# Softmax sums spread by TensorE, and the merge's other loads issued by ScalarE, in a hybrid decoder layer

## The chip, the cores and the metric

The kernel runs on 1 core of one Trainium2 chip. The metric is the device time of one execution in microseconds (us), lower is better. A core has TensorE (PE, the matrix array; PEld are its weight loads), VectorE (DVE), ScalarE (ACT), GpSimd (POOL) and SyncE (SP), each with a queue that it works through in order, and 16 DMA engines that move data between DRAM and SBUF. SyncE computes nothing here; its queue issues transfers. ScalarE, too, can issue transfers from its queue, between its computations. A matrix product is written to PSUM, eight banks of 128 x 512 numbers; whoever reads a bank sets it free.

## What is computed

One decoder layer of a sequence of 1024 tokens of width 1024: a SwiGLU half step, two token mixers side by side (a gated delta rule, and sparse attention with 8 heads), their merge by sigmoid gates, the output projection, a second half step. Of the reference, cut to what this change touches:

```python
logits = jnp.einsum('bqhr,bqkr->bqhk', q_lat, c_sel) * (SA_DH ** -0.5) + bias
p = jax.nn.softmax(logits, axis=-1)
o_lat = jnp.einsum('bqhk,bqkr->bqhr', p, c_sel)
o_sa = jnp.einsum('bqhr,rhd->bqhd', o_lat, w_uv).reshape(B, Q_BLOCK, SA_W)
...
merged = jax.nn.sigmoid(gate_a) * o_dn + jax.nn.sigmoid(gate_b) * o_sa
x = x + merged @ w_o
```

All of it is in float32; the kernel makes a product of two float32 matrices from three products of their rounded parts (`mm3`: high x high, high x low, low x high).

## The kernel before

The stage in question is the sparse attention, from about 1610 to 1900 us. It goes over 8 heads, in pairs that share one load of value weights (w_uv, `attn_values`: eight products into vh and vl). For each head, query and key are projected from the latents (`attn_qk`, PSUM tag qk, products named pqk): weights w_uq and w_uk are loaded through the two slots of w_raw, cast to a high part by ScalarE and split by GpSimd (wa), multiplied, and evicted by ScalarE and VectorE (p). The call of `ahead()` at step 1 projects the next head while this one runs.

`attn_head` then takes the queries in four groups g of 256, in the order 0, 1, 3, 2. For a group: GpSimd adds the bias of near keys to a mask (nb); TensorE multiplies queries by keys (pl, three banks); VectorE adds the mask and takes the row maximum (a_mx, a_nm); ScalarE takes the exponential and sums each row (a_sum); TensorE transposes the probabilities in blocks (pp, two banks, tag pt); ScalarE and VectorE evict them in parts (ph, plo); TensorE multiplies them by the values (pao, one bank); ScalarE copies the result to osa. There the head's channel is on the partitions and the query along the row, while a_sum has the query on the partitions. So the reciprocal sums r of a half head (512 queries, 128 x 4 numbers) must be turned into a row and spread over all partitions.

`merge` does that after groups 1 and 2, once per half head. It loads three tiles of 128 x 512 with one buffer each: od (the other mixer's result, `odd`), zg and gb (gates, `zgd` and `gbd`). It stores r to DRAM (a_rd), and loads it back as a row for every partition (a_rb, one buffer). For the very last half head it uses TensorE instead: four diagonal matrices made by VectorE (a_d), multiplied by ones (a_rp). What `merge` returns, `done`, is called one group later for the first half and two groups later for the second: GpSimd multiplies od by zg, VectorE multiplies osa by the spread sums and gate, GpSimd adds both into the row merged[hd] (mr).

All these loads and the store leave from SyncE's queue, and so do the weights (line 1256), the near bias (line 584) and then w_o (line 132). The order of instructions on each engine is set when the program is built, by a scheduler that plays the program in a model of time; `issue_after` keeps an instruction from being put ahead of another one, and `high_priority` lets the projection go up to 1600 instructions ahead. After the heads the merged rows are split in two parts (mh by ScalarE, ml by VectorE and GpSimd), and the output projection follows (pwo).

Of the kernel before, what the change touches and what calls it, by code (L numbers as in the profile page):

```python
# [10 lines left out]
F32 = mybir.dt.float32  # L11
F32R = mybir.dt.float32r
# [3 lines left out]
ALU = mybir.AluOpType  # L16
# [4 lines left out]
P = 128  # L21
D = 1024
S = 1024
# [47 lines left out]
class Layer:  # L71
# [1188 lines left out]
    def attn_values(self, pair, p, ps):  # L1260
        nc = self.nc
        wh, wl = self.attn_weights(self.I["w_uv"][0][:, 2 * pair:2 * pair + 2, :].rearrange("r h d -> r (h d)"), 256, p, "wuv")
        vh = p.tile([P, NT, 256], F32R, name="vh", tag="vh", bufs=1)
        vl = p.tile([P, NT, 256], F32R, name="vl", tag="vl", bufs=1)
        for t in range(0, NT, 2):
            pv = ps.tile([P, 2, 256], F32, name="pav", tag="qk")
            for i in range(2):
                for k in range(2):
                    lh, ll = (x[2 + k][t // 4][:, ts((t + i) % 4, P)] for x in self.lat)
                    self.mm3(pv[:, i, :], lh, ll, wh[:, k, :], wl[:, k, :], k == 0, k == 1)  # L1270
            nc.scalar.copy(vh[:, t:t + 2, :], pv)
            nc.vector.tensor_sub(vl[:, t:t + 2, :], pv, vh[:, t:t + 2, :])
        return vh, vl
# [20 lines left out]

    def attn_head(self, hd, p, ps, qk, values, merged, ahead):
        nc = self.nc
# [4 lines left out]
        sums = self.stat.tile([P, NT], F32, name="a_sum")  # L1301
        osa = p.tile([P, S], F32, name="osa", tag="osa", bufs=2)
        for g in (0, 1, 3, 2):
            probs = []
            for b in (2 * g, 2 * g + 1):
# [24 lines left out]
            for j in range(0, 2 * g + 2, 2):  # L1330
# [3 lines left out]
                for i, (jj, b) in enumerate(blocks):  # L1334
                    nc.tensor.transpose(pt[:, ts(i, P)], probs[b][:, ts(jj, P)], self.ident)
                ph = p.tile([P, 512], F32R, name="ph", tag="ph", bufs=3)
# [3 lines left out]
                for i in range(2):  # L1340
                    a, b = (0, 256) if i == 0 else (256, n)
                    out = po[:, 0:256] if b - a == 256 else po[:, 128:256]
                    self.mm3(out, vh[:, j + i, hv], vl[:, j + i, hv], ph[:, a:b], pl_[:, a:b], j + i == 0, j + i == 2 * g + 1)
            nc.scalar.copy(osa[:, ts(g, 256)], po[:, 0:256])
            if g == 1:
                ahead()
            for late in self.outs:
                late[0] -= 1
            while self.outs and self.outs[0][0] == 0:
                with self.tc.issue_after(dve.ins):  # L1350
                    self.outs.pop(0)[1]()
            if g in (1, 2):
                out = self.merge(hd, g // 2, sums, osa, p, ps, merged)
                if hd == H - 1 and g == 2:
                    out()
                else:
                    self.outs.append([g, out])

    def merge(self, hd, h, sums, osa, p, ps, merged):
# [5 lines left out]
        nc.vector.tensor_scalar_mul(r, r, 0.5)  # L1365
        od, zg, gb = (p.tile([P, 512], F32, name=n, tag=n, bufs=1) for n in ("od", "zg", "gb"))
        v = ts(h, 512)
        for x, src in ((od, self.odd[hd][:, v]), (zg, self.zgd[hd][:, v]), (gb, self.gbd[hd][:, v])):
            nc.sync.dma_start(x, src)
        if hd == H - 1 and h == 1:  # L1370
            rb = ps.tile([P, 512], F32, name="a_rp", tag="pt")
            for t in range(4):
                d = p.tile([P, P], F32, name="a_d", tag="near", bufs=2)
                nc.vector.tensor_scalar_mul(d, self.ident, r[:, t:t + 1])
                nc.tensor.matmul(rb[:, ts(t, P)], lhsT=self.ones, rhs=d, start=True, stop=True)
        else:
            rd = self.dram.tile([512], F32, name="a_rd", tag="a_rd", bufs=2)
            nc.sync.dma_start(rd.rearrange("(t i) -> i t", i=P), r)
            rb = p.tile([P, 512], F32, name="a_rb", tag="a_rb", bufs=1)
            nc.sync.dma_start(rb, rd.partition_broadcast(P))  # L1380

        def done():
            nc.gpsimd.tensor_mul(od, od, zg)
            nc.vector.tensor_mul(osa[:, v], osa[:, v], rb)
            nc.vector.scalar_tensor_tensor(osa[:, v], gb, 1.0, osa[:, v], ALU.add, ALU.mult)
            nc.gpsimd.tensor_add(merged[:, v], od, osa[:, v])

        return done

# [139 lines left out]
    def mixer(self, hs):  # L1529
# [3 lines left out]
        with ExitStack() as km:  # L1533
# [79 lines left out]
            with ExitStack() as c:  # L1613
# [5 lines left out]

                def ahead():  # L1620
                    if len(qk) < H:
                        with self.tc.high_priority(offset=AHEAD):
                            qk.append(self.attn_qk(len(qk), (p, "wqk", 2), ps))

                for i in range(H):
                    if i % 2 == 0:
                        vals = self.attn_values(i // 2, p, ps)
                    self.attn_head(i, p, ps, qk[i], vals, raw[i], ahead)
                hs.close()
# [55 lines left out]
```

## Time and profile before

| | |
|---|---|
| time, 3 runs | 2646.43, 2651.6 (median), 2653.45 us |
| the profiled execution | 2654.08 us, span 2652.1 us |
| PE busy | 2519.1 us, 95% of the span |
| DVE, ACT, POOL busy | 66%, 45%, 37% |
| granted TensorE clock, mean | 0.971 of full |

The span goes from the first to the last instruction of the profiled execution. Busy shares are means over the whole kernel, most of which is other stages; what this change can move is in the 290 us of the attention. The granted clock is a share of 2.4 GHz; the array has two levels, 2.4 and 1.2 GHz, and a mean between them says for how much of a stretch each held.

### The profile page before, as it was taken

The numbers are of one execution on the slowest core, as the hardware profiler recorded it, in microseconds if no ns is written. First come the engines' busy times: TensorE is split into PE (matmuls) and PEld (weight loads), VectorE is DVE, ScalarE is ACT, GpSimd is POOL, SyncE is SP. The second block draws the span as 40 slices with busy tenths as digits, with TensorE's granted clock in tenths as the row PEclk, the third lists the DMA queues.
The fourth block names the chain that finished last, engine by engine and source line by source line (L and its number), as shares of the span: only waits on it lengthen the run. The fifth ranks groups of instructions, "written<-read, shape, count | busy, mean of one in ns | idle before, by whom it ended". The sixth has DMA issues, their size and how long they took to land.

```text
span 2652.1 us, 36132 instructions
## 1 busy us (share of the span) xinstructions
PE 2519.1 (95%) x12526; PEld 2054.9 (77%) x12526; DVE 1737.9 (66%) x3424; ACT 1198.3 (45%) x2338; POOL 970.9 (37%) x748
## 2 busy tenths in 40 slices
PE   6999999999999899989999999779898999999998
PEld 5788888888787688777778778678776888888886
DVE  7655555676555677999566866566668555546676
ACT  6444344333434665544368446445434434434333
POOL 5555444343434233332100002333446545543340
PEclk8999999999999899999999999889998999999999
DMA  5443346753444155445633323333632344347642
GB/s 168 136 143 129 113 146 219 255 194 101 120 114 122 41 140 139 115 124 123 200 124 116 124 82 74 82 76 78 200 111 94 102 143 143 127 150 263 224 151 75
DMA packets 375607, 356.67 MB, mean 134 GB/s; under 512 B 95417, under 2 KB 279553, under 8 KB 374401
## 3 DMA queue, kind: packets, MB, share of 16 engines
q1 hardware_dynamic: 371840, 348.60, 42.1%
q10 hardware_dynamic: 2304, 4.20, 0.4%
q0 software_dynamic: 1280, 1.57, 0.3%
q8 instruction: 99, 1.62, 0.3%
q14 instruction: 84, 0.68, 0.1%
HBM read 238.28 MB, written 116.01 MB: 134 GB/s over the span
## 4 chain that ended last, share of the span: by engine, by line
PE 40%; DVE 9%; DMA 6%; issue 2%; ACT 1%; POOL 1%; SPq 0%; DVEq 0%; POOLq 0%; ACTq 0%
PE pst L139 7%; PE pst L141 7%; PE pst L140 7%; PE pin L141 2%; PE pin L139 2%; PE pin L140 2%; DVE sb_p L1034 2%; DMA a_rd<-a_r 2%; DMA od<-odd 1%; PE pn L1221 1%; PE po L1230 1%; PE pv L1216 1%; DVE cv_y L923 1%; PE pq L1211 1%; PE pwo L141 1%
## 5 line engine op out<-in xcount | busy, mean ns | idle before, releaser
L140 PE MATMUL pst<-p,w_hi 128*128 128x512 f32 x992 | 392.1, 395 | 8.6 <-DVE p L112 8.5
L139 PE MATMUL pst<-p,w_hi 128*128 128x512 f32 x992 | 393.2, 397 | 4.1 <-ACT p L111 2.3
L141 PE MATMUL pst<-p,w_hi 128*128 128x512 f32 x992 | 391.3, 395 | 0.5 <-DVE w_hi L112 0.5
L139 PE MATMUL pin<-p,w_hi 128*128 128x512 f32 (+1 forms) x848 | 342.1, 405 | 6.0 <-DVE cv_y L923 4.2
L111 ACT CAST w_hi<-w_raw 128x512 fp32r<-128x512 f32 (+3 forms) x294 | 204.1, 695 | 311.7 <-PE pst L141 135.8
L140 PE MATMUL pin<-p,w_hi 128*128 128x512 f32 (+1 forms) x848 | 340.5, 402 | 0.5 <-DVE p L112 0.5
L141 PE MATMUL pin<-p,w_lo 128*128 128x512 f32 (+1 forms) x848 | 340.8, 402 | 0.0
L112 DVE TENSOR_TENSOR w_lo<-w_raw,w_lo 128x512 fp32r<-128x512 f32 (+1 forms) x196 | 188.3, 963 | 167.2 <-ACT w_lo L111 165.6
L140 PE MATMUL pst<-p,w_lo 128*128 128x512 f32 x744 | 292.7, 394 | 3.7 <-DVE p L112 3.7
L141 PE MATMUL pst<-p,w_lo 128*128 128x512 f32 x744 | 292.2, 393 | 1.2 <-DVE w_lo L112 1.2
L139 PE MATMUL pst<-p,w_lo 128*128 128x512 f32 x744 | 290.6, 396 | 0.5 <-ACT c L360 0.5
L140 PEld LDWEIGHTS pst<-p,w_hi 128*128 128x128 f32 x992 | 188.3, 190 | 53.9 <-DVE p L112 12.9
L139 PEld LDWEIGHTS pst<-p,w_hi 128*128 128x128 f32 x992 | 188.8, 190 | 47.3 <-ACT p L111 3.5
L141 PEld LDWEIGHTS pst<-p,w_hi 128*128 128x128 f32 x992 | 188.5, 190 | 43.0 <-DVE w_hi L112 1.3
L111 ACT CAST w_lo<-w_raw 128x512 fp32r<-128x512 f32 (+1 forms) x200 | 115.7, 582 | 207.4 <-PE pst L141 97.8
L139 PEld LDWEIGHTS pin<-p,w_hi 128*128 128x128 f32 (+1 forms) x848 | 161.6, 191 | 42.7 <-DVE cv_y L923 4.5
L141 PEld LDWEIGHTS pin<-p,w_lo 128*128 128x128 f32 (+1 forms) x848 | 161.5, 190 | 37.7 <-issue 3.8
L140 PEld LDWEIGHTS pin<-p,w_hi 128*128 128x128 f32 (+1 forms) x848 | 161.6, 191 | 37.5 <-issue 4.0
L373 DVE TENSOR_TENSOR c<-c,pst 128x512 f32<-128x512 f32 x132 | 89.9, 682 | 150.9 <-PE pst L141 118.1
L112 POOL TENSOR_TENSOR w_lo<-w_raw,w_hi 128x1024 fp32r<-128x1024 f32 (+1 forms) x43 | 107.0, 2488 | 199.4 <-ACT w_hi L111 189.4
L140 PEld LDWEIGHTS pst<-p,w_lo 128*128 128x128 f32 x744 | 140.7, 189 | 35.1 <-DVE p L112 4.9
L141 PEld LDWEIGHTS pst<-p,w_lo 128*128 128x128 f32 x744 | 140.7, 189 | 33.5 <-DVE w_lo L112 2.1
(427 smaller groups left out, 5393.8 us busy)
## 6 DMA issues: line engine op xcount, KB each, us to landing
p<-mixd SPq DMA_DIRECT2D x144, 256.0 KB, 5.4
w_raw<-in_w_in_dram SPq DMA_DIRECT2D x52, 512.0 KB, 4.1
w_raw<-in_ffn_wg_dram SPq DMA_DIRECT2D x44, 512.0 KB, 3.6
w_raw<-in_ffn_wu_dram SPq DMA_DIRECT2D x44, 512.0 KB, 4.0
mixd<-t_hi SPq DMA_DIRECT2D x72, 256.0 KB, 4.3
mixd<-t SPq DMA_DIRECT2D x72, 256.0 KB, 3.8
w_raw<-in_ffn_wd_dram SPq DMA_DIRECT2D x48, 384.0 KB, 4.1
actd<-c SPq DMA_DIRECT2D x70, 256.0 KB, 2.0
```

The source lines that it names most:

```text
L111: self.nc.scalar.copy(hi, raw)
L112: self.pin((self.nc.vector if engine == "vector" else self.nc.gpsimd).tensor_sub(lo, raw, hi))
L139: mm(ps, lhsT=wh, rhs=rh, start=first, stop=False, **kw)
L140: mm(ps, lhsT=wh, rhs=rl, start=False, stop=False, **kw)
L141: mm(ps, lhsT=wl, rhs=rh, start=False, stop=last, **kw)
L373: nc.vector.tensor_add(c[i, h], c[i, h], bank["y" if m == 1 else "z"])
L923: nc.vector.scalar_tensor_tensor(y[:, n:512], pps[h][:, 0:512 - n], cw[:, j:j + 1], y[:, n:512], ALU.mult, ALU.add)
L1034: nc.vector.tensor_mul(v, T[:, 0:i, 0:i].rearrange("p j c -> p c j"), L[:, None, 0:i, i].to_broadcast([P, i, i]))
L1211: nc.tensor.matmul(pq[:, i, :], lhsT=kq[:, h, ts(c, P)], rhs=old[:, h, :], start=True, stop=True)
L1216: nc.tensor.matmul(pv[r, i, :], lhsT=X[r, h, :], rhs=vb[r, h, :], start=True, stop=True)
L1221: nc.tensor.matmul(pn[:, i, :], lhsT=kd[r, h, :], rhs=vn[r, h, :], start=True, stop=True)
L1230: nc.tensor.matmul(po[r, i, :], lhsT=at[r, h, :], rhs=vn[r, h, :], start=True, stop=True)
```

## The change

The reciprocal sums no longer go through DRAM: `spread`, which the kernel has for its norms, makes four products of r (each column repeated 128 times, as the weights) with the identity, into a bank of tag pt (n_rb), from which VectorE multiplies osa. This is used for every half head, the last included. `merge` becomes a generator: its first step takes the reciprocals and issues the load of gb (now two buffers) from ScalarE's queue; its second, one group later, does the rest. The other mixer's part is a generator of its own, `other_branch`: it loads the whole row of odd for a head straight into the merged row, and the gate zg by halves (one buffer), from ScalarE's queue, and GpSimd multiplies in place, one group after each load. GpSimd then adds osa (for the last half head VectorE does). The tiles osa, vh and vl are cut into two and four, so that a part can be freed earlier.

```diff
--- before.py
+++ after.py
@@ -1260,16 +1260,15 @@
     def attn_values(self, pair, p, ps):
         nc = self.nc
         wh, wl = self.attn_weights(self.I["w_uv"][0][:, 2 * pair:2 * pair + 2, :].rearrange("r h d -> r (h d)"), 256, p, "wuv")
-        vh = p.tile([P, NT, 256], F32R, name="vh", tag="vh", bufs=1)
-        vl = p.tile([P, NT, 256], F32R, name="vl", tag="vl", bufs=1)
+        vh, vl = ([p.tile([P, 2, 256], F32R, name=n, tag=f"{n}{t}", bufs=1) for t in range(NT // 2)] for n in ("vh", "vl"))
         for t in range(0, NT, 2):
             pv = ps.tile([P, 2, 256], F32, name="pav", tag="qk")
             for i in range(2):
                 for k in range(2):
                     lh, ll = (x[2 + k][t // 4][:, ts((t + i) % 4, P)] for x in self.lat)
                     self.mm3(pv[:, i, :], lh, ll, wh[:, k, :], wl[:, k, :], k == 0, k == 1)
-            nc.scalar.copy(vh[:, t:t + 2, :], pv)
-            nc.vector.tensor_sub(vl[:, t:t + 2, :], pv, vh[:, t:t + 2, :])
+            nc.scalar.copy(vh[t // 2], pv)
+            nc.vector.tensor_sub(vl[t // 2], pv, vh[t // 2])
         return vh, vl

     def attn_qk(self, hd, p, ps):
@@ -1292,15 +1291,16 @@
             qk.append((hi, lo))
         return qk

-    def attn_head(self, hd, p, ps, qk, values, merged, ahead):
+    def attn_head(self, hd, p, ps, qk, values, merged, ahead, other):
         nc = self.nc
         near = self.near_tile(p, hd)
         (qh, ql), (kh, kl) = qk
         vh, vl = values
         hv = slice((hd % 2) * P, (hd % 2) * P + P)
         sums = self.stat.tile([P, NT], F32, name="a_sum")
-        osa = p.tile([P, S], F32, name="osa", tag="osa", bufs=2)
         for g in (0, 1, 3, 2):
+            if g in (0, 3):
+                osa = p.tile([P, 512], F32, name="osa", tag="osa", bufs=2)
             probs = []
             for b in (2 * g, 2 * g + 1):
                 W = (b + 1) * P
@@ -1332,7 +1332,7 @@
                 blocks = [(j, 0), (j, 1), (j + 1, 0), (j + 1, 1)] if j < 2 * g else [(j, 0), (j, 1), (j + 1, 1)]
                 n = len(blocks) * P
                 for i, (jj, b) in enumerate(blocks):
-                    nc.tensor.transpose(pt[:, ts(i, P)], probs[b][:, ts(jj, P)], self.ident)
+                    pe = nc.tensor.transpose(pt[:, ts(i, P)], probs[b][:, ts(jj, P)], self.ident)
                 ph = p.tile([P, 512], F32R, name="ph", tag="ph", bufs=3)
                 pl_ = p.tile([P, 512], F32R, name="plo", tag="plo", bufs=3)
                 nc.scalar.copy(ph[:, 0:n], pt[:, 0:n])
@@ -1340,21 +1340,21 @@
                 for i in range(2):
                     a, b = (0, 256) if i == 0 else (256, n)
                     out = po[:, 0:256] if b - a == 256 else po[:, 128:256]
-                    self.mm3(out, vh[:, j + i, hv], vl[:, j + i, hv], ph[:, a:b], pl_[:, a:b], j + i == 0, j + i == 2 * g + 1)
-            nc.scalar.copy(osa[:, ts(g, 256)], po[:, 0:256])
-            if g == 1:
-                ahead()
-            for late in self.outs:
-                late[0] -= 1
-            while self.outs and self.outs[0][0] == 0:
-                with self.tc.issue_after(dve.ins):
-                    self.outs.pop(0)[1]()
-            if g in (1, 2):
-                out = self.merge(hd, g // 2, sums, osa, p, ps, merged)
-                if hd == H - 1 and g == 2:
-                    out()
-                else:
-                    self.outs.append([g, out])
+                    self.mm3(out, vh[j // 2][:, i, hv], vl[j // 2][:, i, hv], ph[:, a:b], pl_[:, a:b], j + i == 0, j + i == 2 * g + 1)
+            act = nc.scalar.copy(osa[:, ts(g % 2, 256)], po[:, 0:256])
+            ahead(hd, g)
+            with self.tc.issue_after(dve.ins), self.tc.issue_after(act.ins), self.tc.issue_after(pe.ins):
+                for out in self.outs:
+                    next(out, None)
+                if g in (1, 2):
+                    out = self.merge(hd, g // 2, sums, osa, p, ps, merged)
+                    next(out)
+                    self.outs = self.outs[-1:] + [out]
+                other(hd, g)
+            if hd == H - 1 and g == 2:
+                for out in self.outs:
+                    for _ in out:
+                        pass

     def merge(self, hd, h, sums, osa, p, ps, merged):

@@ -1363,29 +1363,27 @@
         r = self.stat.tile([P, 4], F32, name="a_r")
         nc.vector.reciprocal(r, sums[:, ts(h, 4)])
         nc.vector.tensor_scalar_mul(r, r, 0.5)
-        od, zg, gb = (p.tile([P, 512], F32, name=n, tag=n, bufs=1) for n in ("od", "zg", "gb"))
         v = ts(h, 512)
-        for x, src in ((od, self.odd[hd][:, v]), (zg, self.zgd[hd][:, v]), (gb, self.gbd[hd][:, v])):
-            nc.sync.dma_start(x, src)
-        if hd == H - 1 and h == 1:
-            rb = ps.tile([P, 512], F32, name="a_rp", tag="pt")
-            for t in range(4):
-                d = p.tile([P, P], F32, name="a_d", tag="near", bufs=2)
-                nc.vector.tensor_scalar_mul(d, self.ident, r[:, t:t + 1])
-                nc.tensor.matmul(rb[:, ts(t, P)], lhsT=self.ones, rhs=d, start=True, stop=True)
-        else:
-            rd = self.dram.tile([512], F32, name="a_rd", tag="a_rd", bufs=2)
-            nc.sync.dma_start(rd.rearrange("(t i) -> i t", i=P), r)
-            rb = p.tile([P, 512], F32, name="a_rb", tag="a_rb", bufs=1)
-            nc.sync.dma_start(rb, rd.partition_broadcast(P))
-
-        def done():
-            nc.gpsimd.tensor_mul(od, od, zg)
-            nc.vector.tensor_mul(osa[:, v], osa[:, v], rb)
-            nc.vector.scalar_tensor_tensor(osa[:, v], gb, 1.0, osa[:, v], ALU.add, ALU.mult)
-            nc.gpsimd.tensor_add(merged[:, v], od, osa[:, v])
-
-        return done
+        last = hd == H - 1 and h == 1
+        gb = p.tile([P, 512], F32, name="gb", tag="gb", bufs=2)
+        nc.scalar.dma_start(gb, self.gbd[hd][:, v])
+        yield
+        rb = self.spread(r, p, ps, "pt")
+        nc.vector.tensor_mul(osa, osa, rb)
+        nc.vector.scalar_tensor_tensor(osa, gb, 1.0, osa, ALU.add, ALU.mult)
+        (nc.vector if last else nc.gpsimd).tensor_add(merged[:, v], merged[:, v], osa)
+
+    def other_branch(self, hd, p, merged):
+
+        nc = self.nc
+        nc.scalar.dma_start(merged, self.odd[hd])
+        for h in range(2):
+            v = ts(h, 512)
+            zg = p.tile([P, 512], F32, name="zg", tag="zg", bufs=1)
+            nc.scalar.dma_start(zg, self.zgd[hd][:, v])
+            yield
+            nc.gpsimd.tensor_mul(merged[:, v], merged[:, v], zg)
+            yield


     def out_proj(self, m, ps, after_tile, after_half):
@@ -1617,15 +1615,23 @@
                 raw = [mlp.tile([P, S], F32, name=f"mr{k}", tag=f"mr{k}") for k in range(NK)]
                 qk = self.qk

-                def ahead():
-                    if len(qk) < H:
+                others = [self.other_branch(k, p, raw[k]) for k in range(H)]
+                next(others[0])
+
+                def other(hd, g):
+                    for k, at in ((hd, (0, 1, 3)), (hd + 1, (2,))):
+                        if k < H and g in at:
+                            next(others[k], None)
+
+                def ahead(hd, g):
+                    if hd + 1 < H and g == 1:
                         with self.tc.high_priority(offset=AHEAD):
-                            qk.append(self.attn_qk(len(qk), (p, "wqk", 2), ps))
+                            qk.append(self.attn_qk(hd + 1, (p, "wqk", 2), ps))

                 for i in range(H):
                     if i % 2 == 0:
                         vals = self.attn_values(i // 2, p, ps)
-                    self.attn_head(i, p, ps, qk[i], vals, raw[i], ahead)
+                    self.attn_head(i, p, ps, qk[i], vals, raw[i], ahead, other)
                 hs.close()
                 mp = self.pool(ms, "merged", 1, "right")
                 hi, lo = ([mp.tile([P, S], F32R, name=f"{n}{k}", tag=f"{n}{k}") for k in range(NK)] for n in ("mh", "ml"))
```

What that does to the queues, at three places. SyncE's queue, around the load of the third pair of heads' value weights (w_uv); od, zg, gb, a_rd and a_rb are the merge's transfers. Before:

```order
L1369 DMA od<-odd 128x512
L1369 DMA zg<-zgd 128x512
L1380 DMA a_rb<-a_rd 128x512
L1369 DMA gb<-gbd 128x512
L1369 DMA od<-odd 128x512
L1378 DMA a_rd<-a_r 128x4x1
L1369 DMA zg<-zgd 128x512
L1256 DMA w_raw<-in_w_uv_dram 128x2x256
L1380 DMA a_rb<-a_rd 128x512
L1369 DMA gb<-gbd 128x512
L1256 DMA w_raw<-in_w_uq_dram 128x2x128
L1369 DMA od<-odd 128x512
```

and now:

```order
L1256 DMA w_raw<-in_w_uq_dram 128x2x128
L584 DMA near<-nb_wide 128x256
L1256 DMA w_raw<-in_w_uk_dram 128x2x128
L584 DMA near<-nb_wide 128x256
L1256 DMA w_raw<-in_w_uv_dram 128x2x256
L1256 DMA w_raw<-in_w_uq_dram 128x2x128
L1256 DMA w_raw<-in_w_uk_dram 128x2x128
L1256 DMA w_raw<-in_w_uq_dram 128x2x128
```

The weights and the near bias stay; nothing of the merge is between them any more.

ScalarE's queue, ahead of the cast of the same value weights (wa 128x512); vh, ph, osa and p are evictions, ACTIVATE with a_sum the exponentials. Before:

```order
L1344 COPY osa<-pao 128x256
L1327 ACTIVATE w_lo,a_sum<-w_lo,a_nm 128x768
L1288 ACTIVATE p_10_15129<-pqk 128x512
L1288 ACTIVATE p_10_15140<-pqk 128x512
L111 CAST wa<-w_raw 128x256
L1338 CAST ph<-pp 128x512
L1338 CAST ph<-pp 128x384
L1288 ACTIVATE p_10_15151<-pqk 128x512
L111 CAST wa<-w_raw 128x512
L1288 ACTIVATE p_10_15162<-pqk 128x512
```

and now:

```order
L1344 COPY osa<-pao 128x256
L1369 DMA gb<-gbd 128x512
L1379 DMA mr_14141<-odd 128x1024
L1383 DMA zg<-zgd 128x512
L1270 CAST vh<-pav 128x512
L1327 ACTIVATE w_hi,a_sum<-w_hi,a_nm 128x896
L1338 CAST ph<-pp 128x512
...
L111 CAST wa<-w_raw 128x512
L1287 ACTIVATE p_10_15182<-pqk 128x512
L111 CAST wa<-w_raw 128x256
L1344 COPY osa<-pao 128x256
L1369 DMA gb<-gbd 128x512
L1383 DMA zg<-zgd 128x512
```

Loads of gb, of a whole row of odd (into mr) and of zg now stand between an eviction and the next exponentials.

TensorE's queue, at one of the 16 spreads (n_rb), with the products of probabilities and values (pao) and logits (pl) around it. Now:

```order
L139 MATMUL pao<-ph,vh 128x256
L140 MATMUL pao<-plo,vh 128x256
L141 MATMUL pao<-ph,vl 128x256
L179 MATMUL n_rb<-ident,a_r 128x128 x4
L139 MATMUL pao<-ph,vh 128x256
L139 MATMUL pl<-p_10_15549,p_10_15527 128x384
L140 MATMUL pl<-p_11_15550,p_10_15527 128x384
L141 MATMUL pl<-p_10_15549,p_11_15528 128x384
```

Before, no product of this kind stood there; only the last half head had its four (a_rp).

## Rows read from the trace of the kernel before

**Rows 1.** The page's head.

```profile
span 2652.1 us, 36132 instructions
```

**Rows 2.** Stretches: us, busy us of each engine (instructions), PEclk, DMA share, GB/s.

```profile
core 0: us, PE busy (x) PEld busy (x) DVE busy (x) ACT busy (x) POOL busy (x), PEclk, DMA share, GB/s
1620.00:1660.00 40.00, 40.00 (x271) 36.51 (x270) 29.50 (x94) 23.53 (x54) 13.45 (x17) 1.00 0.29 60
1660.00:1680.00 20.00, 14.76 (x96) 13.28 (x94) 11.64 (x46) 8.02 (x21) 4.48 (x7) 0.83 0.15 46
1680.00:1700.00 20.00, 18.87 (x135) 17.28 (x133) 12.18 (x31) 12.21 (x26) 8.12 (x10) 1.00 0.39 102
1700.00:1720.00 20.00, 9.11 (x30) 7.13 (x31) 6.03 (x18) 5.02 (x13) 5.72 (x6) 0.57 0.37 90
1720.00:1770.00 50.00, 47.86 (x332) 43.22 (x330) 36.44 (x116) 27.59 (x64) 19.02 (x24) 1.00 0.35 75
1770.00:1790.00 20.00, 8.52 (x27) 6.90 (x28) 6.07 (x18) 5.02 (x13) 6.09 (x6) 0.59 0.32 79
1790.00:1810.00 20.00, 20.00 (x134) 18.32 (x134) 14.84 (x54) 11.81 (x29) 8.95 (x13) 0.99 0.28 73
1810.00:1850.00 40.00, 34.73 (x232) 30.84 (x230) 27.78 (x83) 19.74 (x45) 10.18 (x11) 0.96 0.37 73
1850.00:1880.00 30.00, 21.72 (x117) 17.71 (x116) 23.75 (x55) 18.15 (x36) 14.21 (x12) 0.89 0.33 88
```

**Rows 3.** TensorE's waits, 1600 to 1910: total us, times, longest us.

```profile
PE pqk L139 <- DVE p L1289: 22.2, 4, 9.1
PE pl L139 <- DVE a_mx L1322: 9.9, 3, 5.1
```

**Rows 4.** The chain that ended last, at the first long gap: start, us, what.

```profile
1698.59 3.21 DMA od<-odd
...
1701.99 1.24 POOL od L1383
1703.23 0.69 POOL wa L112
...
1703.94 9.19 DMA w_raw<-in_w_uv_dram
...
1715.04 0.79 PE pqk L139
```

**Rows 5.** Waits in SyncE's queue, 1600 to 1910: total us, times, longest us.

```profile
SPq L1369 <- POOL od L1383: 91.0, 15, 12.5
SPq L1380 <- DMA a_rd<-a_r: 85.2, 12, 11.2
```

**Rows 6.** Waits of the other engines, 1580 to 1910: total us, times, longest us.

```profile
POOL od L1383 <- DMA od<-odd: 62.3, 9, 14.7
...
ACT wa L111 <- DMA w_raw<-in_w_uv_dram: 36.5, 3, 17.7
...
DVE osa L1384 <- DMA a_rb<-a_rd: 26.7, 9, 6.3
```

**Rows 7.** The page's DMA issues: count, KB each, median us to landing.

```profile
od<-odd SPq DMA_DIRECT2D x16, 256.0 KB, 6.0
...
w_raw<-in_w_uv_dram SPq DMA_DIRECT2D x4, 256.0 KB, 6.9
```

**Rows 8.** Groups of instructions, 1590 to 1905: shapes, count, busy us, mean ns.

```profile
L1384 DVE TENSOR_TENSOR osa<-osa,a_rb 128x512 f32<-128x512 f32 x15 | 11.0, 730 | 26.7 <-DMA a_rb<-a_rd 26.7
...
L1375 PE MATMUL a_rp<-a_d,ones 128*128 128x128 f32 x8 | 1.2, 274 | 0.0
...
L1384 DVE TENSOR_TENSOR osa<-osa,a_rp 128x512 f32<-128x512 f32 x1 | 0.7, 689 | 0.0
```

**Rows 9.** The chain, at the last half head's spread.

```profile
1888.79 0.44 PE a_rp L1375 x4
...
1894.60 0.44 PE a_rp L1375 x4
```

**Rows 10.** ScalarE's own transfers (a gate's store): count, ns min/median/max, first and last start.

```profile
L1125 ACTq DMA_DIRECT2D gbd<-tb x16: 326/326/338, 808.2 to 1591.0; - x16
```

## The prediction

> **What bounds the kernel now.** I read the profile's head first [rows 1]: one core, 2652.1 us of span. The same execution took 2654.1 us, so 2.0 us lie around the span, and the median of the runs shown, 2651.6, is 2.5 below it. The diff touches only the sparse-attention stage, so next comes the table of stretches [rows 2], read by two columns: PE busy and PEclk, the granted TensorE clock as a share of 2.4 GHz. At 1620 to 1660 us the array has no gap and full clock, and at 1790 to 1810 nearly so: where it is fed, TensorE bounds this stage. Between 1660 and 1880 it is not always fed. Length less PE busy gives the idle time: 5.24, 1.13, 10.89, 2.14, 11.48, 0, 5.27 and 8.28 us, 44.4 in all. The clock falls where the gaps are: it averages 0.57 and 0.59 around the two long ones, so part of those stretches ran at 1.2 GHz. What that cost is at most busy time times (1 - PEclk): 2.5, 3.9, 3.5, 0.2, 1.4 and 2.4 us in the stretches below 1.00, 13.9 together. So 58.3 us are to be had in this stage if nothing were added.
>
> TensorE's own waits say what it lacked [rows 3]: 22.2 us for the q/k projection of the next head (pqk), whose PSUM bank is freed by VectorE's split (p), and 9.9 us for a bank of logits that VectorE had still to reduce (a_mx). Neither is slow arithmetic. The chain through the first long gap [rows 4] shows why: the od load lands, GpSimd multiplies od by zg, only then comes its weight split (wa), only then can SyncE issue the next value weights (w_uv), which land 9.19 us later; ScalarE, in order, has been standing at their cast, and the pqk evictions stand behind it. The queue views agree. SyncE waits 91.0 us for od to be multiplied and 85.2 us for the sums to land in DRAM before it can send them back spread [rows 5]; GpSimd waits 62.3 us for od, ScalarE 36.5 us for w_uv (17.7 the longest), VectorE 26.7 us for a_rb (6.3 the longest) [rows 6]. It is one loop through SyncE's queue: od, zg, gb and a_rb have one buffer each, so the loads of one half head wait for the merge of the half before, the merge waits for two transfers in sequence, and the weights wait in the same queue.
>
> **The change part by part.**
>
> *SyncE's queue is emptied of the merge.* What leaves it: 15 stores a_rd, 15 spread loads a_rb and 48 loads of od, zg, gb. The order shows the place of the first gap: the w_uv load had gb, od, a_rd and zg ahead of it, and now has weights and near tiles only. It still waits until GpSimd has split an earlier weight, since w_raw has two slots, and GpSimd is still in order; but the od x zg product now stands a step of the loop behind its loads. So the w_uv load starts right after a weight split of 0.69 us [rows 4] and lands in 6.9 us [rows 7]: ScalarE waits at most 7.6 us for it. It waited 17.7, and TensorE idled 10.89, so TensorE's work covered 6.8. That leaves 0.8 us a gap; I leave 2.0 for both. The two gaps of 22.4 us with their 7.4 us of clock then give back **27.8 us** (bounds: 0, if GpSimd still arrives late, and 29.8).
>
> *The sums are spread by TensorE.* VectorE no longer waits for a_rb. Its longest such wait (6.3) covers TensorE's wait of 5.1 us for a_mx in 1660 to 1680, a stretch that lost 5.24 + 2.5 = 7.7; I take **6.5** back, 1.2 staying (bounds 0 and 7.7). The price is four products a spread; the kernel has that already for its last half head, written differently. Those show as two records a product of 274 ns each that overlap [rows 8], and the chain gives 0.44 us for four records [rows 9], so 0.88 us a spread. There are 15 new ones, and one replaces the old: **13.2 us** if TensorE is never idle where they stand, nothing if all fall into gaps. In the order they stand between pao products of full stretches, so I take all 13.2. A spread also holds one of two pt banks until VectorE has read it, as a transpose does; no row shows what that costs, and I put it into the bounds of the next sum (0 to one VectorE pass of 0.69 [rows 8] for each of 15, 10 us). VectorE's multiplication keeps its time: it read PSUM in 689 ns for the last half head, against a mean of 730 from SBUF [rows 8].
>
> *1850 to 1880* lost 8.28 + 2.4 = 10.7. The loop's last rounds are in it, but also the splitting of all merged tiles for the output projection on VectorE (23.75 of 30 us busy), which stays. I take half, **5** (0 and 10.7). *The rest* (1680 to 1700, 1720 to 1770, 1790 to 1850) lost 8.5 idle and 1.6 clock; the last heads have no projection left to fill the gaps. I take **2** (0 and 10.1). The smaller tiles for vh, vl and osa (a half or a quarter freed earlier) work in these two terms and get nothing of their own.
>
> *ScalarE issues 40 loads* (16 gb, 16 zg, 8 whole rows of odd). One issue of this kind takes 326 ns on its queue [rows 10], 13 us in all; ScalarE is busy for 24 of 40 us in the first stretch and 18 of 30 in the last [rows 2], so that hides, and if it did not it would cost 13. What does not hide is a load that has to wait while exponentials stand behind it. The first odd load must see the last odd store land, issued ahead of it; od's landing of 6.0 us [rows 7] bounds that, once; I take 2. Each zg load waits for GpSimd's product of the half before, two steps of the loop earlier; I take 1 for all. Together **3** (0 to 6 + 13).
>
> GpSimd does the same 32 passes less one, VectorE four small ones less and one more: off the path, nothing.
>
> Sum: 27.8 + 6.5 + 5 + 2 - 13.2 - 3 = 25.1 us. 2654.1 - 25.1 = 2629.0 for a profiled execution, and 2.5 less for the median: **2626.5 us**.
>
> One rule speaks against half of this. The Trainium skill, page DMA: Bandwidth & Descriptors, section "Issuing engines are not separate DMA queues", says that transfers started by SyncE and by ScalarE run on the same 16 engines, and that using both saves only the time of issuing. By that the 48 loads would give back their issue time, off the path here, and the transfers would land as late as now. The trace so far shows a queue that stands still for 91.0 and 85.2 us rather than one busy issuing [rows 5]. What the rule would make of the time is the second rival.
>
> **The rivals.**
>
> 1. *TensorE becomes the only bound.* All 58.3 us come back and only the spreads are paid: 2654.1 - 45.1 - 2.5 = **2606.5**. For it: the full stretches of 1620 to 1660 and 1790 to 1810 show that the engines can feed it. Against: the tail heads and the final splits have nothing to do with SyncE.
> 2. *The loads are late whoever issues them.* If od and w_uv land late because of the transfers themselves (in the chain, 3.21 and 9.19 us are transfers, not queueing [rows 4]), GpSimd and ScalarE wait as before, and the two long gaps stay. Then 13.5 - 13.2 - 3 = -2.7: **2654.3**, no change. For it: w_uv is only 256 KB and took 9.19. Against: of ScalarE's wait of 17.7 us [rows 6] only 9.19 are this landing, the rest is a load not yet issued, and it lands in 6.9 by the median [rows 7]. By the rule of the Trainium skill named above, this is the case that would come.
> 3. *ScalarE takes the place of SyncE* (slower). A zg load that waits for GpSimd's product stops ScalarE, not an idle queue: exponentials, evictions of pqk and the ph casts stand behind it, VectorE and TensorE behind these, and GpSimd's masks wait for VectorE. Priced by the wait that GpSimd has for od now: 62.3 us, all of it passed on to TensorE: 25.1 - 62.3 = -37.2, **2688.8**. It decides from 33 us on (25 and the 8 that count as slower), about 2.1 us for each of 16 zg loads. For it: one zg buffer, and queues in order. Against: in the order at least seven ScalarE computations stand between a zg load and the next, so GpSimd has some microseconds for a product whose data had been asked for a step before.
>
> **How the numbers follow.** The forecast gets 0.60, rival 1 0.15, rival 2 0.13, rival 3 0.12. The forecast's own range is 2611 to 2642 (the 13.2 and 10.1 that may be won more, the two 5 to 7 us terms and the pt bank that may be lost). The range for 8 in 10 begins at rival 1's time and ends a little short of rival 2's, **2606 to 2652**: above it lie rival 3 and somewhat more than half of rival 2, 0.2 together. A change of 0.3%, 8 us, is about what a measurement of this kernel tells from none. Faster: 0.60 and 0.15 and a little of rival 2, **0.77**; within 0.3%: most of rival 2 and the weak end of the forecast, **0.12**; slower: **0.11**.
>
> **What the profile after would show.** Right: PE busy near the whole length in every stretch of 20 us from the stage's start to its final splits, PEclk 1.00 there; pqk's wait under 4 us; SyncE's waits for od and a_rd gone; ScalarE's wait at w_uv's cast 8 us or less; 128 more records of L179, at about 274 ns. Wrong: ScalarE waiting by GpSimd at its own zg issues for more than 2 us each (rival 3); ScalarE still 15 us at w_uv's cast (rival 2); or TensorE waiting for pt banks or at the spreads for a_r. The prediction fails on size if the final splits or the tail heads take the idle time over, and in sign only by rival 3.

## The result, and the profile after

Before, 2652.52 us (median of 4 runs, 2646.43 to 2653.8); after, 2619.05 us (median of 4, 2616.99 to 2619.7). The ratio is 0.9877 (95% interval 0.986 to 0.9894): 33.5 us less, where 25.1 had been forecast, inside the forecast's own range. Timed again later with more runs, the kernel after took 2618.36 us and the kernel before 2640.11, ratio 0.9918 (0.99 to 0.9937), 21.7 us less. The kernel after gave the same time on both occasions; the kernel before did not. The sections below compare experiments with the later times: 2618.4 for after, and 2638.8 to 2641.7 for before beside each of them. One execution of all, 3558.2 us at a granted clock of 0.646, in the run of od without its buffer, is left out.

The head of the page of the kernel after, and its stretches as in [rows 2] (us, busy us of PE, PEld, DVE, ACT, POOL, PEclk, DMA share, GB/s):

```profile
span 2617.7 us, 36275 instructions
```

```profile
1620.00:1820.00 200.00, 197.16 (x1369) 180.79 (x1368) 143.44 (x465) 116.70 (x267) 81.10 (x98) 1.00 0.22 70
1820.00:1850.00 30.00, 25.12 (x129) 21.00 (x128) 23.72 (x46) 17.49 (x34) 13.44 (x9) 0.89 0.27 88
1850.00:1880.00 30.00, 30.00 (x153) 25.42 (x152) 15.83 (x20) 11.76 (x17) 7.07 (x6) 1.00 0.70 235
```

TensorE is idle for 2.84 us in the 200 us up to 1820, at full clock. What is left stands at the final splits, 1820 to 1850: 4.88 us idle and at most 25.12 x 0.11 = 2.8 us of clock. Together 10.5 us, where [rows 2] held 58.3.

Waits in the kernel after, 1590 to 1890 (total us, times, longest us), the answer to [rows 3, 5, 6]:

```profile
PE pao L140 <- DVE plo L1339: 4.0, 6, 2.0
PE pot L1190 <- ACT o L1185: 3.3, 1, 3.3
...
PE pl L139 <- DVE a_mx L1322: 0.8, 2, 0.6
```

```profile
SPq L1256 <- POOL wa L112: 73.8, 15, 17.3
...
SPq L584 <- POOL nb L1309: 47.2, 6, 20.6
```

```profile
POOL mr L1385 <- DMA zg<-zgd: 23.5, 8, 9.8
...
ACT wa L111 <- DMA w_raw<-in_w_uv_dram: 0.7, 1, 0.7
```

The pqk wait of 22.2 us is gone, SyncE has run ahead and waits mostly for slots (of weights and of the near bias), ScalarE's wait at w_uv's cast fell from 36.5 to 0.7. Its transfers also land sooner (kernel after, transfers issued from 1590 to 1890, median us to landing last):

```profile
zg<-zgd ACTq DMA_DIRECT2D x16, 256.0 KB, 3.8
...
gb<-gbd ACTq DMA_DIRECT2D x16, 256.0 KB, 2.8
...
w_raw<-in_w_uv_dram SPq DMA_DIRECT2D x3, 256.0 KB, 2.7
```

w_uv needed 6.9 before [rows 7]. A quieter queue should start a transfer earlier, not make it shorter; that is the first sign that the prediction had the wrong cause. The second stood in the trace of before, unread. Call **the bounce** the way of the reciprocal sums through DRAM: store, wait, spread load. Its store, 2 KB, is the slowest transfer of the stage, and the chain went through it (kernel before; transfers as above, then three of the five longest pieces of the chain in 1620 to 1880):

```profile
a_rd<-a_r SPq DMA_DIRECT2D x15, 2.0 KB, 11.5
```

```profile
1727.77 11.67 DMA a_rd<-a_r
1753.47 10.99 DMA a_rd<-a_r
1809.79 13.07 DMA a_rd<-a_r
```

At the first of the three TensorE was still fed (47.86 of 50 us busy in [rows 2]); the second leads into the second long gap. The chain there, and one row of SyncE's queue, in order of time:

```profile
1753.47 10.99 DMA a_rd<-a_r
1764.51 0.32 SPq L1380
...
1765.40 5.55 DMA od<-odd
...
1773.08 9.90 DMA w_raw<-in_w_uv_dram
```

```profile
1765.83 0.42 SPq L1378 DMA_DIRECT2D a_rd<-a_r  x1
```

The store costs in two ways. SyncE could issue the spread load (L1380), and behind it gb and od, only when the store had landed, after 10.99 us. And od and w_uv, issued beside the next store, took 5.55 and 9.90 us. So a part of the store's cost did pass through SyncE's queue; no run shows how much went each way.

### The profile page after: what moved, and what is told of

Read it like the earlier page. It is cut to its first block, busy times and chain, and to the rows that moved or that the text cites. A ratio compares the mean times of both kernels' runs of the same rounds, so it can differ in the third digit from the quotient of the medians.

```text
span 2617.7 us, 36275 instructions
## 1 busy us (share of the span) xinstructions
PE 2524.6 (96%) x12646; PEld 2065.4 (79%) x12646; DVE 1730.5 (66%) x3421; ACT 1200.7 (46%) x2338; POOL 968.6 (37%) x747
## 4 chain that ended last, share of the span: by engine, by line
PE 48%; DVE 8%; ACT 1%; issue 1%; DMA 1%; DVEq 0%; ACTq 0%; SPq 0%
PE pst L141 7%; PE pst L139 7%; PE pst L140 7%; PE pin L141 2%; PE pin L140 2%; PE pin L139 2%; DVE sb_p L1034 1%; PE po L1230 1%; PE pv L1216 1%; PE pn L1221 1%; DVE cv_y L923 1%; PE pq L1211 1%; PE pwo L140 1%; PE pwo L141 1%; PE pwo L139 1%; PE pp L1335 1%
## 5 line engine op out<-in xcount | busy, mean ns | idle before, releaser
L112 DVE TENSOR_TENSOR w_lo<-w_raw,w_lo 128x512 fp32r<-128x512 f32 (+1 forms) x196 | 193.8, 991 | 167.2 <-ACT w_lo L111 165.2
```

Source lines behind the costliest of these rows:

```text
L112: self.pin((self.nc.vector if engine == "vector" else self.nc.gpsimd).tensor_sub(lo, raw, hi))
```

## Experiments

Theory of the prediction: the gaps came from **the queue**, where loads with one buffer stood ahead of weight loads. Rival A, the second of the prediction: the loads are late whoever issues them. Rival B, formed after the trace of after had been read: **the bounce** itself. After the first four runs B was sharpened to **the store of single elements**, 512 packets of 4 bytes, which holds back every transfer near it.

**The loads back on SyncE.** The kernel after, with

```diff
-        nc.scalar.dma_start(gb, self.gbd[hd][:, v])
+        nc.sync.dma_start(gb, self.gbd[hd][:, v])
```

and the same for odd and zg.

> The changed kernel, but the 40 loads of gb, odd and zg are issued by SyncE again; the spreads stay on TensorE and the smaller tiles stay. My theory (the long gaps came from a queue in which weight loads stood behind loads that wait for a buffer): the zg loads, with their one buffer, again stand ahead of weight loads; SyncE waits tens of us for GpSimd's product, ScalarE stands at the cast of w_uv again, and most of the 33.5 us are lost: 2640 to 2660. Rival A (the Trainium skill, page DMA: Bandwidth & Descriptors: two issuing engines save issue time only): 2619 +/- 3, since the issue time was hidden anyway. Rival B (it was the bounce through DRAM that held SyncE): 2619 to 2625, since the bounce is still gone.

Measured: 2613.47 us (2612.95 to 2620.27), ratio 0.9904 (0.9887 to 0.9921): 4.9 below the kernel after, not above it. Two of its five executions took 2619 and 2620, as the kernel after does, so the 4.9 are not clear of noise. SyncE again waits, 66.2 us for a gb buffer and 19.0 for GpSimd's product, and ScalarE still waits only 3.4 us at w_uv's cast:

```profile
SPq L1369 <- DVE osa L1373: 66.2, 8, 15.4
...
SPq L1383 <- POOL mr L1385: 19.0, 14, 1.8
```

```profile
ACT wa L111 <- DMA w_raw<-in_w_uv_dram: 3.4, 2, 2.5
```

The queue theory fails its first test: these waits in the queue are harmless, since what stands behind them is still early. In this run only zg has one buffer, so the run of the spread alone, below, is the fuller test.

**The bounce back, the loads on ScalarE.** The kernel after, with

```diff
-        yield
-        rb = self.spread(r, p, ps, "pt")
+        if last:
+            yield
+            rb = self.spread(r, p, ps, "pt")
+        else:
+            rd = self.dram.tile([512], F32, name="a_rd", tag="a_rd", bufs=2)
+            nc.sync.dma_start(rd.rearrange("(t i) -> i t", i=P), r)
+            rb = p.tile([P, 512], F32, name="a_rb", tag="a_rb", bufs=1)
+            nc.sync.dma_start(rb, rd.partition_broadcast(P))
+            yield
```

> The changed kernel, but for 15 of 16 half heads the reciprocals go through DRAM again (store and spread load issued by SyncE, one buffer a_rb, as before the change); the other loads stay on ScalarE. My theory: TensorE saves 15 x 0.88 = 13.2 us of spreads, the long gaps stay small because the od and zg loads no longer stand in that queue, but SyncE waits for each a_rd store to land with weight loads behind it, and VectorE for a_rb: 2606 + 5 to 15, so 2611 to 2621. Rival B (the bounce made the gaps: SyncE's 85.2 us at a_rd): the gaps come back, 2635 to 2650.

Measured: 2736.85 us (2735.47 to 2737.88), ratio 1.0359 (1.0344 to 1.0375): 118 us above the kernel after, far outside both. Its transfers, 1600 to 1880, and its waits, 1590 to 1890:

```profile
zg<-zgd ACTq DMA_DIRECT2D x12, 256.0 KB, 11.1
...
gb<-gbd ACTq DMA_DIRECT2D x11, 256.0 KB, 11.0
...
a_rd<-a_r SPq DMA_DIRECT2D x11, 2.0 KB, 9.9
```

```profile
POOL mr L1392 <- DMA zg<-zgd: 71.5, 7, 12.5
DVE osa L1379 <- DMA a_rb<-a_rd: 70.7, 8, 13.7
```

gb and zg leave from the other engine's queue and land in 11 us beside the store, against 2.8 and 3.8 without it. VectorE, in order, stands for 70.7 us at the product with a_rb, and TensorE behind it (25.4 us for logits that VectorE had still to reduce).

**Each product of the spread twice.** The kernel after, with each of the four products of a merge's spread issued two times.

> The changed kernel, each product of the merge's spreads issued twice (the second overwrites the first with the same numbers). If TensorE has no idle time where the spreads stand (my 13.2 us for 15): 16 x 0.88 = 14.1 us more, 2633. If spreads fall into gaps: 0 to 5 more, 2619 to 2624.

Measured: 2631.91 us (2627.93 to 2634.94), ratio 0.9961 (0.9948 to 0.9974): 13.5 above the kernel after, for 14.1 expected. The spreads are paid in full.

**The spread by a transpose.** The kernel after, with

```diff
-        rb = self.spread(r, p, ps, "pt")
+        rb = ps.tile([P, 512], F32, name="n_rb", tag="pt")
+        for t in range(4):
+            nc.tensor.transpose(rb[:, ts(t, P)], r[:, t:t + 1].to_broadcast([P, P]), self.ident)
```

> The changed kernel, the merge's spreads done by a transpose of the broadcast column in place of a product with the identity. In the trace an f32 transpose is one record where the product is two, 0.11 us apart each. If the stage is bound by TensorE: 16 x 0.44 = 7.0 us less, 2612. If the spreads lie in gaps, or a transpose of a column that is repeated is no cheaper: 2619 +/- 2.

Measured: 2610.64 us (2608.52 to 2614.59), ratio 0.9884 (0.9868 to 0.99): 7.7 below the kernel after, for 7.0 expected. The groups by line (shapes, count, busy us, mean ns), kernel after and then this one, show half the instruction records at the same length:

```profile
L179 PE MATMUL n_rb<-ident,a_r 128*128 128x128 f32 x128 | 18.1, 286 | 0.0
```

```profile
L1373 PE MATMUL n_rb<-ident,a_r 128*128 128x128 f32 x64 | 10.1, 283 | 0.0
```

**The kernel after once more.**

> The changed kernel as it is, as the base for the others of this call and of the call before. Ratio to before 0.986 to 0.9894 as at first; if this chip gives another ratio, the others are read against this one.

Measured: the 2618.36 us given at the start (2617.64 to 2626.89).

**The spread alone.** The kernel before, the bounce replaced in all half heads; queue, single buffers and order stay:

```diff
...
-            rd = self.dram.tile([512], F32, name="a_rd", tag="a_rd", bufs=2)
-            nc.sync.dma_start(rd.rearrange("(t i) -> i t", i=P), r)
...
-            nc.sync.dma_start(rb, rd.partition_broadcast(P))
...
         def done():
             nc.gpsimd.tensor_mul(od, od, zg)
+            rb = self.spread(r, p, ps, "pt")
```

> The kernel before, with only the spread changed: all 16 half heads are spread by four products on TensorE; od, zg and gb stay in SyncE's queue with one buffer each, as does the order of the merge. Theory of the prediction (the loop od load, product, weight load in SyncE's queue made the long gaps): they stay, 13 us of spreads are paid, only the 85.2 us of SyncE's waits at a_rd and the wait for a_rb go: ratio 0.997 to 1.003. Rival B, that the loads on SyncE (2613 against 2637 to 2650 forecast) have made likelier: the bounce held the queue, and its store of single elements the other transfers; without it the gaps close and od lands in 4 us or less instead of 6.0: ratio 0.988 to 0.993.

Measured: 2617.01 us (2610.67 to 2620.17), ratio 0.9906 (0.9885 to 0.9927). That is the whole change (the kernel after, timed beside it, has 0.9918), and it is what rival B expected, with all the single buffers still in SyncE's queue. Waits and transfers, 1590 to 1890:

```profile
SPq L1369 <- POOL od L1372: 48.0, 15, 4.6
```

```profile
POOL od L1372 <- DMA od<-odd: 15.6, 9, 3.0
...
ACT wa L111 <- DMA w_raw<-in_w_uv_dram: 3.1, 3, 1.7
```

```profile
od<-odd SPq DMA_DIRECT2D x16, 256.0 KB, 2.8
...
w_raw<-in_w_uv_dram SPq DMA_DIRECT2D x3, 256.0 KB, 2.9
```

The same loads from the same queue land in less than half the time of [rows 7], and SyncE still waits 48.0 us for GpSimd's product without harm: by themselves the single buffers and the loads in that queue make no long gap.

**The bounce in fewer packets.** The kernel before, with the store as r lies in SBUF, 16 bytes a partition, and the reordering in VectorE's read:

```diff
-            nc.sync.dma_start(rd.rearrange("(t i) -> i t", i=P), r)
+            nc.sync.dma_start(rd.rearrange("(i t) -> i t", i=P), r)
...
-            nc.vector.tensor_mul(osa[:, v], osa[:, v], rb)
...
+                o = osa[:, v].rearrange("p (t i) -> p t i", i=P)
+                nc.vector.tensor_mul(o, o, rb.rearrange("p (i t) -> p t i", i=P))
```

> The kernel before, but the bounce's store is written as it lies in SBUF, 16 bytes a partition (128 packets in place of 512 of 4 bytes), and VectorE reads the spread row in strides in place of the store's reordering. Queues, buffers and order stay. If the many small packets are what makes the bounce land late (a_rd 5.9 us by the median in the kernel before, 9.9 in the run with the bounce beside ScalarE's loads): a_rd lands in 4 us or less and 10 us or more are won, ratio 0.990 to 0.996. If it is the round trip and the queue whatever the packets: ratio 0.998 to 1.002; a strided read that is slower on VectorE would show in the mean of its product (730 ns before).

(The 5.9 us in it is a median over the store and the spread load together; the store alone is the 11.5 shown above.) Measured: 2606.4 us (2603.33 to 2609.63), ratio 0.9866 (0.9845 to 0.9887). The layout of one store in the kernel before, with a strided read to match, wins 33.7 us, 12 more than the change and more than the range expected. The pages' counts of packets, kernel before and then this one, show the edit: 5761 fewer under 512 bytes, and 15 stores x 384 are 5760.

```profile
DMA packets 375607, 356.67 MB, mean 134 GB/s; under 512 B 95417, under 2 KB 279553, under 8 KB 374401
```

```profile
DMA packets 369846, 356.67 MB, mean 137 GB/s; under 512 B 89656, under 2 KB 273792, under 8 KB 368640
```

Transfers, 1590 to 1890, and the product's group:

```profile
od<-odd SPq DMA_DIRECT2D x16, 256.0 KB, 2.7
...
w_raw<-in_w_uv_dram SPq DMA_DIRECT2D x3, 256.0 KB, 3.2
a_rd<-a_r SPq DMA_DIRECT2D x15, 2.0 KB, 2.4
```

```profile
L1389 DVE TENSOR_TENSOR osa<-osa,a_rb 128x512 f32<-128x512 f32 x15 | 17.4, 1157 | 0.0
```

The store lands in 2.4 us, everything near it about as fast as without a bounce; the strided read costs VectorE 1157 ns instead of 730 [rows 8], and TensorE, which pays no spreads but the last, has no wait for pqk. The 12 us to the kernel after are near the 13.2 of the spreads.

**od without its buffer.** The kernel before, od loaded into the result tile, zg with two buffers, the bounce as before:

```diff
-        od, zg, gb = (p.tile([P, 512], F32, name=n, tag=n, bufs=1) for n in ("od", "zg", "gb"))
         v = ts(h, 512)
+        od = merged[:, v]
+        zg, gb = (p.tile([P, 512], F32, name=n, tag=n, bufs=b) for n, b in (("zg", 2), ("gb", 1)))
```

> The kernel before, but od is loaded straight into the head's own result tile (no buffer to wait for) and zg gets two buffers; the bounce and the queue stay. Theory of the prediction: SyncE no longer waits for GpSimd's product (91.0 us), the two long gaps (10.89 and 11.48 us) shrink: ratio 0.990 to 0.995. Rival B (the bounce alone): SyncE's waits move to a_rd and a_rb, ratio 0.998 to 1.002.

Measured: 2644.39 us (median of eleven, 2639.52 to 2652.61), ratio 1.0014 (1.0001 to 1.0028). The loop that the prediction had blamed is opened at od and zg, and nothing is won, as rival B expected. What SyncE no longer waits for GpSimd, it waits at the store:

```profile
SPq L1381 <- DMA a_rd<-a_r: 108.3, 13, 10.9
```

**A store that nobody reads.** The kernel after, and between its gb and zg loads

```diff
+        rd = self.dram.tile([512], F32, name="a_rd", tag="a_rd", bufs=2)
+        nc.scalar.dma_start(rd.rearrange("(t i) -> i t", i=P), r)
```

> The changed kernel, and for each of 16 half heads the old store of r to DRAM (512 elements of 4 bytes) is issued again, by ScalarE between the loads of gb and zg; nothing reads it and no load waits for it but by sharing the transfer engines. If the store of single elements slows the other transfers: zg lands in 8 us or more instead of 3.8 (11.1 in the run with the bounce in the changed kernel), GpSimd waits for it, w_uv lands later; 2625 to 2660. If the harm came only from SyncE and VectorE waiting for the round trip: 2618 +/- 4 with zg at 4 us or so.

Measured: 2672.92 us (2667.73 to 2674.79), ratio 1.011 (1.0089 to 1.0131): 54.6 above the kernel after, more than the range expected, for 16 stores of 2 KB whose data goes nowhere. Transfers and waits, 1590 to 1890:

```profile
zg<-zgd ACTq DMA_DIRECT2D x16, 256.0 KB, 10.8
mr<-odd ACTq DMA_DIRECT2D x8, 512.0 KB, 12.3
gb<-gbd ACTq DMA_DIRECT2D x15, 256.0 KB, 3.7
...
near<-nb_wide SPq DMA_DIRECT2D x8, 128.0 KB, 2.1
...
w_raw<-in_w_uv_dram SPq DMA_DIRECT2D x3, 256.0 KB, 3.2
...
a_rd<-a_r ACTq DMA_DIRECT2D x15, 2.0 KB, 10.0
```

```profile
POOL mr L1387 <- DMA zg<-zgd: 109.5, 15, 15.6
...
ACT ph L1338 <- POOL mr L1387: 22.2, 6, 6.4
```

What is issued behind the store (mr, zg) lands with it; what went ahead (gb) and what leaves at other times (near, two of three w_uv) hardly changes. The third w_uv left SyncE's queue 4.4 us behind a store that ScalarE had issued, and took 8.7 us. So the round trip isn't needed for the harm in this kernel. And here the prediction's third rival is seen alive: zg comes late, GpSimd's product late, and ScalarE waits 22.2 us at its own zg issues with the ph casts behind.

**The bounce in fewer packets, in the kernel after.** The run of 2736.85 us with the layout of the run of 2606.4.

> The changed kernel with the bounce back on SyncE as in the run that took 2737 us, but stored in 128 packets of 16 bytes and read in strides by VectorE, as in the kernel before with fewer packets (2606). If the packets made that run slow: a_rd lands in 2 to 4 us instead of 9.9, zg and gb in 4 instead of 11, and the time is 2602 to 2612, since no spreads are paid. If the place of the bounce in the changed kernel's order is to blame (VectorE waits for a_rb soon after r): 2650 or more still.

Measured: 2627.2 us (2621.36 to 2641.81), ratio 0.9951 (0.9933 to 0.997). That is in neither of the two ranges expected: 110 of the 118 us go with the packets (zg lands in 4.7 us, a_rd in 1.8), but 21 us above the same bounce in the kernel before remain: VectorE still waits 17.4 us for a_rb and GpSimd 38.8 for zg. By argument, up to 1 MB of loads leaves just beside the bounce in this order; no run separated that.

**Fewer packets and od without its buffer.** The two edits shown above together, in the kernel before.

> A candidate for the best: the kernel before with the bounce in 128 packets, od loaded straight into the result tile and two zg buffers. With the bounce cheap, SyncE's remaining waits are for GpSimd's product (47.1 us in the run with fewer packets) and are taken away; TensorE's waits there are small, so little is to be won: 2600 to 2608 against 2606.4. If single buffers still cost: 2598 or less.

Measured: 2607.18 us (2600.9 to 2608.09), ratio 0.9859 (0.9842 to 0.9877): the same as with fewer packets alone, as expected.

**Loads on SyncE and the transpose.** Both edits shown above together, in the kernel after.

> The changed kernel with both edits that made it faster: gb, odd and zg are issued by SyncE again (2613.5 us by itself) and the merge's spreads are transposes (2610.6 by itself, 7.7 below the changed kernel). If the two are independent: 2613.5 - 7.7 = 2606, the time of the kernel before with fewer packets (2606.4), without a trip through DRAM. If the gain of the loads on SyncE is an accident of the order: 2609 to 2613.

Measured: 2610.99 us (2604.41 to 2612.93), ratio 0.9884 (0.9865 to 0.9904). The two gains don't add: with the transpose, the loads on SyncE win nothing (2610.64 without them, ratio 0.9884 both times), so their own 4.9 us may be no gain at all.

## Why the prediction came out

The sum was near, and a cause in it was wrong. That the number came out is in part luck: most of the gain was booked under the loads, and it came from the other part of the change, which was made together with them. By the prediction's steps:

- *"SyncE's queue is emptied of the merge"*, 27.8 us: the gaps closed and the size holds, but the departure of the loads did nothing. The spread alone closes them (2617.0), and with the loads back on SyncE they stay closed (2613.5). Of all that the term lists as leaving the queue, the 15 stores with their spread loads carried the gain. The failed step stands ahead of the sum: "It is one loop through SyncE's queue: od, zg, gb and a_rb have one buffer each". With od's and zg's buffers out of that loop the time stayed (1.0014). What stood in its place was the store of 512 single elements: with all of the loop kept and only that store in fewer packets, the time fell to 2606.4. The term also took w_uv's landing of 6.9 us as given; without the store it is 2.7.
- *"The sums are spread by TensorE"*, 6.5 won and 13.2 paid: the 13.2 was right (13.5 for 16 spreads doubled, 7.7 back for half of each). The gain of this part was mis-sized, since the removal of the bounce carried the whole result, the long gaps included.
- *"1850 to 1880"*, 5: the final splits keep 4.88 + 2.8 = 7.7 of 10.7; 3.0 came back. *"The rest"*, 2: 200 us up to 1820 lose 2.84, so nearly all of the 10.1 came back. In all 58.3 - 10.5 = 47.8 of the stage returned, for 41.3 forecast; less 13.2 that is 34.6, and the spans differ by 34.4. All this is read from one execution of the kernel before, of 2654.08 us; on the later occasion it took 2640.11, and no trace shows where those 14 us lay.
- *"ScalarE issues 40 loads"*, 3: nothing left of the difference for it; its issues show no waits in the kernel after. The 4.9 us of the run with the loads on SyncE would fit it, but are not clear of noise.
- The pt bank (0 to 10): no wait of TensorE for one is among its waits; the low end held.
- *Rival 2*: its rule, the Trainium skill, page DMA: Bandwidth & Descriptors, section "Issuing engines are not separate DMA queues", was right about the half that it speaks of. Moving 40 loads to another engine's queue bought no time (2618.4 with, 2617.0 and 2613.5 without). The rival was also right that the transfers themselves were slow. Its time failed because they were not slow by nature: without the store od and w_uv land in 2.7 to 2.9 us. The Trainium skill, same page, section "Specifications", says that transfers under 512 bytes make the DMA engine read, modify and write. That no run here shows; the trace agrees that small packets are slow (11.5 us for 2 KB in 4-byte packets), but packets of 16 bytes are under that limit too, and 128 of them land in 2.4.
- *Rival 3*: not in the kernel after; its mechanism appears once zg is made late (22.2 us, above).

The expected signs all came (no pqk wait, 0.7 us at w_uv's cast, 128 records of L179), and all of them would have come by rival B as well: they tested the outcome, not the cause. Only the landing times told the two apart, and the prediction named none.

What stays open: whether the number or the size of the packets does it, since the edit changed both; how much of the store's cost in the kernel before came through SyncE's wait for it, and how much through slower transfers beside it; whether the loads on SyncE are faster at all; and the 21 us of the bounce in the order after.

## What to carry to other kernels

Read the landing time of each transfer against its bytes before blaming a queue: 2 KB in 11.5 us is the finding, and the chain named that store. A store whose layout breaks it into single elements was paid here by its neighbours, too; change the layout first (2606.4, one line and a strided read), and move the work to another engine second (2618.4), since a bound engine charges for it. When two parts of a change go together, give each a run of its own: here half of the change, and the reason given for it, did nothing.

## What the runs showed of the hardware

- A store of 2 KB in 512 packets of 4 bytes took 9.4 to 11.5 us to land (medians of four runs), in 128 of 16 bytes 1.8 to 2.4 (three runs): about a fifth.
- Big loads issued close to such a store land with it, from the same queue (10.8 and 12.3 us) and from another (11.0). In the run of 2736.85 us one zg issue of 13, made beside a store, lasted 3.54 us on ScalarE's queue, where the median is 0.37; why, no run shows.

```profile
1629.93 3.54 ACTq L1390 DMA_DIRECT2D zg<-zgd  x1
```

- An f32 transpose with a column repeated along the free axis spreads that column like the product with the identity, in half the records (64 against 128, of 283 and 286 ns).
- VectorE reading one operand with a stride of 16 bytes took 1157 ns for 128x512, against 730 and 689 unstrided [rows 8].
